# Attention scores of four heads in one step, with 64-row and 32-row products side by side, in a two-layer decoder trunk

## The chip, the cores and the metric

The kernel runs on one core of one Trainium2 chip. The metric is the device time of one launch in microseconds (us); the time given for a kernel is the median of its runs. One run is also recorded with the hardware profiler. Its trace gives each instruction of the engines: TensorE (PE, with its weight loads as PEld), VectorE (DVE), ScalarE (ACT), GpSimd (POOL), and the DMA queue that SyncE (SP) feeds.

## The reference

The reference is a trunk of two decoder layers over 16 learned meta tokens and 256 tokens (L = 272), width 1024. A layer is a half-step SwiGLU feed-forward net, a mixing sub-layer with two branches (latent attention and a gated recurrence, HGRN2), and a second feed-forward net. The last layer computes no queries for the meta tokens, since they are dropped at the end. The change is in the attention branch:

```python
def mla(c_q, c_kv, k_pe, pos, q_norm_w, kv_norm_w, w_uq, w_ukv):
    H, DQK = MLA_HEADS, QK_NOPE + QK_ROPE          # 8 heads, 64 + 32
    q = (rms_norm(c_q, q_norm_w) @ w_uq).reshape(B, L, H, DQK)
    q = jnp.concatenate([q[..., :QK_NOPE], rope(q[..., QK_NOPE:], pos)], axis=-1)
    kv = (rms_norm(c_kv, kv_norm_w) @ w_ukv).reshape(B, L, H, QK_NOPE + V_HEAD)
    v = kv[..., QK_NOPE:]
    k_rot = rope(k_pe[:, :, None, :], pos)
    k = jnp.concatenate([kv[..., :QK_NOPE], jnp.broadcast_to(k_rot, (B, L, H, QK_ROPE))], axis=-1)
    ...
        s = jnp.einsum('bqhd,bkhd->bhqk', qi, k).astype(jnp.float32) * scale
        s = jnp.where(k_pos[None, :] <= q_pos[:, None], s, NEG_BIG)
        p = jax.nn.softmax(s, axis=-1).astype(v.dtype)
        return jnp.einsum('bhqk,bkhd->bqhd', p, v)
```

A score is thus a dot product over 96 numbers: 64 "nope" numbers that each head has for itself, in the queries and in the keys, and 32 "rotary" numbers, whose keys are the same for all heads.

## The kernel before

Activations lie with channels on the 128 partitions and tokens along the free axis. Every weight product is done as three fp32r products of split operands (`mm3`, lines 163 to 165), and the weights stream from memory in pieces of 128 x 1024. `piece()` (line 151) hands out the next piece and prepares the one two further on: an ACT cast (`wh`, line 144) and a DVE subtraction (`wl`, line 145). The attention's own products (scores, transposes, values) and those of the recurrence are plain fp32.

There are eight PSUM banks in two pools of four: "mm" for weight products, "aux" for everything small: scores, transposes of the softmax, the recurrence's blocks.

`mix` (line 398) is one layer's mixing sub-layer. `heads()` (line 474) makes queries, keys and values. For each head it copies the 64 nope rows and the 32 rotary rows into a tile of its own: `qs[hd]` holds rows 0 to 95 of the queries (copies on lines 486 and 500), `kT[hd]` the same of the keys (lines 512 and 513, the second a copy of the shared rotary key `kpe`). `attention()` (line 612) then works head by head. `scores(hd)` does two score products of 96 rows, one for each block of 128 queries (144 and 272 keys), each in an "aux" bank of its own: mask add (642), row maximum (644), exponential with row sum (645), reciprocal (646), scaling of the 16 meta columns into `pmc` (647) and of the rest (650 on ACT, 652 on DVE). `turn(hd)` transposes the probabilities (658 to 660) and copies them to `ptt` (662). In layer 0 alone a small softmax of the 16 meta queries comes first (lines 617 to 632). At the end come the transposes of the meta columns of all heads into `pmt` (675 to 677), and the values in two rounds of two banks: one product of 128 rows with `vt[0]`, a block-diagonal tile of all heads' meta values (682), and the products with the token values (687).

Three generators run interleaved: attention (a), the recurrence (r: `halving()`, then `outputs()`) and weight products (w: the gates' tiles, then projections). `weave("awr", ...)` (line 889) takes one step of each in turn, up to the next `yield`. A scheduler in the compiler orders the instructions within each engine's queue, and each engine then works through its queue in that order. Within the recurrence these places matter: the last products of `halving()` (775 and 778); in `outputs()` the products with meta values (793, 794), the mean square over a head's channels (809, tile `ss`; 811 reads it), its inverse root (lines 283 to 288), and the products that spread it over the partitions (817, "rowsel"), in four "aux" banks, read on line 819.

Of the kernel before, what the change touches and what calls it, by code (L numbers as in the profile page):

```python
# [10 lines left out]
F32 = mybir.dt.float32  # L11
F32R = mybir.dt.float32r
# [15 lines left out]
H = 8  # L28
# [24 lines left out]
def trunk(ctx: ExitStack, tc: tile.TileContext, a: dict):  # L53
# [344 lines left out]
    def mix(l, norm, nxt):  # L398
# [9 lines left out]
        pe = slice(64, 96)  # L408
# [63 lines left out]
        qs, kT, vt = [], [], []  # L472

        def heads():
# [3 lines left out]
            qs.extend(act() for _ in range(H))  # L478
            for pr in range(4):
# [4 lines left out]
                for j in range(2):  # L484
                    js = slice(j * 64, j * 64 + 64)
                    S.copy(out=qs[2 * pr + j][0:NOPE, cq], in_=ps[js, cq])
            yield
            for g in range(2):
# [4 lines left out]
                qp, qw = tmp(), tmp()  # L493
# [4 lines left out]
                for j in range(4):  # L498
                    js = slice(j * 32, j * 32 + 32)
                    S.copy(out=qs[4 * g + j][pe, cq], in_=qp[js, cq])  # L500
# [3 lines left out]
            kT.extend(act() for _ in range(H))  # L504
            for pr in range(4):
# [4 lines left out]
                for j in range(2):  # L510
                    js = slice(j * 64, j * 64 + 64)
                    S.copy(out=kT[2 * pr + j][0:NOPE], in_=ps[js, ca])
                    S.copy(out=kT[2 * pr + j][pe], in_=kpe[0:32])
# [98 lines left out]
        def attention():  # L612
            pmt = act()
            pmc = T([P, 2, P], F32, "pmc", 1)
            sm = T([P, 2, H, 3], F32, "sm", 1)
            if not last:
                ps = PS("aux")
                for hd in range(H):
                    E.matmul(ps[0:NM, hd * NM:(hd + 1) * NM], qs[hd][0:DQK, 0:NM], kT[hd][0:DQK, 0:NM],
                             start=True, stop=True)  # L620
                pmm = T([NM, H, NM], F32, "pmm", 1)
                smm = T([NM, 2, H], F32, "smm", 1)
                V.tensor_tensor(out=pmm, in0=ps[0:NM, 0:P].rearrange("p (h s) -> p h s", s=NM),
                                in1=causal[0:NM, 0:NM].unsqueeze(1).broadcast_to([NM, H, NM]), op=ALU.add)
# [10 lines left out]
            def scores(hd):  # L635
                pms[hd] = [T([P, L], F32, "pm", 4) for _ in range(2)]
                for i, n in enumerate((144, L)):
                    pmx = pms[hd][i]
                    ps = PS("aux")
                    E.matmul(ps[:, 0:n], qs[hd][0:DQK, TOK[i + 1][0]:TOK[i + 1][1]], kT[hd][0:DQK, 0:n],  # L640
                             start=True, stop=True)
# [23 lines left out]
            for hd in range(H):  # L665
                scores(hd)
                if hd:
                    turn(hd - 1)
                yield
# [320 lines left out]
```

## Time and profile before

| | |
|---|---|
| median of 3 runs | 1221.21 us (1219.85 to 1221.59) |
| profiled execution | 1220.78 us |
| its span, first to last instruction | 1218.8 us |
| PE, DVE, ACT busy | 1203.2, 866.9, 645.5 us |
| read from memory | 200.89 MB, 166 GB/s over the span |

The span begins with the first instruction of the program, and the profiled execution is 2.0 us longer. In layer 0 `heads()` runs from about 295 us and the weave of attention, recurrence and gates from 317 to some 375 us; in layer 1 the same parts lie at about 901 and 921 to 976 us. A row of a group (`line engine op out<-in xcount | busy, mean | idle before`) gives the time of all its instructions and the mean of one in ns; a row of the timeline gives start, time, engine, line and operation. A plain fp32 product is one instruction of the program but two in the trace.

### The profile page before, as it was taken

Reading aid. Unit: us, or ns where it says so; the run is one execution under the profiler, and the core shown is the slowest. Engines: PE = TensorE matmul, PEld = TensorE weight load, DVE = VectorE, ACT = ScalarE, POOL = GpSimd, SP = SyncE. Lnnn points to the kernel's source line nnn. Section 1 sums busy time; section 2 is a strip of 40 time slices with the busy share of each in tenths; the row PEclk is TensorE's granted clock in tenths of the full one; section 3 lists DMA queues with packets and bytes.
Section 4 is the critical chain, followed back from the end, with each engine's and each line's share of the span. In section 5 each row is a group of like instructions: output and inputs, shape, how many; then the busy total and the mean of one; then the engine's idle time right before and its main releaser. Section 6 shows DMA issues by size and latency. Waiting matters only on the chain.

```text
span 1218.8 us, 24265 instructions
## 1 busy us (share of the span) xinstructions
PE 1203.2 (99%) x10210; PEld 1170.0 (96%) x10210; DVE 866.9 (71%) x1522; ACT 645.5 (53%) x1067; POOL 8.7 (1%) x19
## 2 busy tenths in 40 slices
PE   7999999999999999999999999999999999999997
PEld 6999999999989999999999999999998899999986
DVE  6877755788786877776558777558877777877643
ACT  5544444575784554444445444445767745544442
POOL 0000000000000000000000000000000000000000
PEclk9999999999999999999999999999999999999999
DMA  7646565544534554646555555556454444655651
GB/s 227 201 149 205 166 189 158 177 143 131 173 105 139 173 163 152 205 153 210 159 165 180 174 173 194 171 173 177 143 151 128 151 156 162 208 173 173 208 190 52
DMA packets 188781, 203.50 MB, mean 167 GB/s; under 512 B 3349, under 2 KB 176481, under 8 KB 188673
## 3 DMA queue, kind: packets, MB, share of 16 engines
q1 hardware_dynamic: 188272, 201.36, 52.0%
q8 instruction: 80, 1.31, 0.5%
q10 hardware_dynamic: 400, 0.60, 0.2%
q14 instruction: 29, 0.23, 0.1%
HBM read 200.89 MB, written 1.05 MB: 166 GB/s over the span
## 4 chain that ended last, share of the span: by engine, by line
PE 96%; DVE 2%; ACT 1%; DMA 0%; issue 0%; SPq 0%; POOLq 0%; POOL 0%
PE pmm L163 22%; PE pmm L164 21%; PE pmm L165 21%; PE paux L164 7%; PE paux L165 7%; PE paux L163 7%; PE pmm L372 2%; PE pmm L373 2%; PE pmm L374 2%; PE paux L640 1%; DVE wl L145 1%; PE paux L711 1%; DMA raw<-x 0%; PE paux L687 0%; PE pmm L376 0%; PE paux L682 0%
## 5 line engine op out<-in xcount | busy, mean ns | idle before, releaser
L144 ACT CAST wh<-raw 128x1024 fp32r<-128x1024 f32 (+3 forms) x398 | 398.4, 1006 | 395.3 <-PE pmm L164 275.6
L145 DVE TENSOR_TENSOR wl<-raw,wh 128x1024 fp32r<-128x1024 f32 (+3 forms) x398 | 465.5, 1173 | 178.9 <-ACT wh L144 176.9
L163 PE MATMUL pmm<-x,wh 128*128 128x272 f32 (+1 forms) x1312 | 382.3, 292 | 0.0
L164 PE MATMUL pmm<-x,wh 128*128 128x272 f32 (+1 forms) x1312 | 376.0, 287 | 0.0
L165 PE MATMUL pmm<-x,wl 128*128 128x272 f32 (+1 forms) x1312 | 375.9, 287 | 0.0
L163 PEld LDWEIGHTS pmm<-x,wh 128*128 128x128 f32 x1312 | 246.7, 188 | 2.2 <-issue 0.7
L164 PEld LDWEIGHTS pmm<-x,wh 128*128 128x128 f32 x1312 | 247.1, 188 | 1.0
L165 PEld LDWEIGHTS pmm<-x,wl 128*128 128x128 f32 x1312 | 246.5, 188 | 0.3
L163 PE MATMUL pmm<-act,wh 128*128 128x272 f32 (+1 forms) x836 | 239.7, 287 | 0.6 <-DVE act L605 0.6
L165 PE MATMUL pmm<-act,wl 128*128 128x272 f32 (+1 forms) x836 | 238.8, 286 | 0.4 <-DVE wl L145 0.4
L164 PE MATMUL pmm<-act,wh 128*128 128x272 f32 (+1 forms) x836 | 238.8, 286 | 0.0
L163 PE MATMUL paux<-x,wh 128*128 128x272 f32 (+1 forms) x704 | 201.1, 286 | 0.0
L164 PE MATMUL paux<-x,wh 128*128 128x272 f32 (+1 forms) x704 | 201.1, 286 | 0.0
L165 PE MATMUL paux<-x,wl 128*128 128x272 f32 (+1 forms) x704 | 201.1, 286 | 0.0
L163 PEld LDWEIGHTS pmm<-act,wh 128*128 128x128 f32 x836 | 157.3, 188 | 0.9 <-DVE act L605 0.8
L165 PEld LDWEIGHTS pmm<-act,wl 128*128 128x128 f32 x836 | 157.0, 188 | 0.6 <-DVE wl L145 0.6
L164 PEld LDWEIGHTS pmm<-act,wh 128*128 128x128 f32 x836 | 157.4, 188 | 0.0
L163 PEld LDWEIGHTS paux<-x,wh 128*128 128x128 f32 x704 | 132.8, 189 | 0.0
L164 PEld LDWEIGHTS paux<-x,wh 128*128 128x128 f32 x704 | 132.6, 188 | 0.0
L165 PEld LDWEIGHTS paux<-x,wl 128*128 128x128 f32 x704 | 132.5, 188 | 0.0
L168 ACT CAST act<-tmp 128x272 fp32r<-128x272 f32 (+1 forms) x88 | 36.5, 415 | 122.5 <-DVE tmp L316 122.5
L312 DVE TENSOR_TENSOR tmp<-pmm,rstd 128x272 f32<-128x272 f32 (+1 forms) x88 | 38.3, 435 | 52.8 <-PE pmm L165 52.7
(249 smaller groups left out, 1037.4 us busy)
## 6 DMA issues: line engine op xcount, KB each, us to landing
raw<-ffn_w_gu SPq DMA_DIRECT2D x86, 1024.0 KB, 5.2
raw<-w_in SPq DMA_DIRECT2D x36, 1024.0 KB, 5.4
raw<-ffn_w_down SPq DMA_DIRECT2D x34, 1024.0 KB, 5.4
raw<-ffn_w_down SPq DMA_DIRECT2D x12, 768.0 KB, 4.9
raw<-w_out SPq DMA_DIRECT2D x8, 1024.0 KB, 5.3
raw<-w_proj_attn SPq DMA_DIRECT2D x4, 1024.0 KB, 5.1
raw<-w_proj_rec SPq DMA_DIRECT2D x4, 1024.0 KB, 5.1
raw<-ffn_w_gu SPq DMA_DIRECT2D x4, 512.0 KB, 8.5
```

The lines of the kernel that those rows point to most:

```text
L144: S.copy(out=hw, in_=x)
L145: V.tensor_tensor(out=lw, in0=x, in1=hw.bitcast(F32), op=ALU.subtract)
L163: E.matmul(ps, wh, xh, start=start, stop=False)
L164: E.matmul(ps, wh, xl, start=False, stop=False)
L165: E.matmul(ps, wl, xh, start=False, stop=stop)
L168: S.copy(out=hi_tile[:, c], in_=src)
L312: V.tensor_tensor(out=gt[:, c], in0=pg[:, c], in1=r[:, c], op=ALU.mult)
L372: E.matmul(pst[t], ah[:, ts_], wh, start=k == 0, stop=False)
L373: E.matmul(pst[t], al[:, ts_], wh, start=False, stop=False)
L374: E.matmul(pst[t], ah[:, ts_], wl, start=False, stop=k == NF - 1)
L640: E.matmul(ps[:, 0:n], qs[hd][0:DQK, TOK[i + 1][0]:TOK[i + 1][1]], kT[hd][0:DQK, 0:n], start=True, stop=True)
L711: E.matmul(pv[32 * b:32 * b + 32, g, ti], k[:, g, bs], q[:, g, bs], start=True, stop=True)
```

## The change

Nothing of the mathematics changes; the score sum is split into its nope and its rotary part.

- **Queries and keys.** No head has tiles of its own any more. `qn[pr]` holds the nope rows of two heads (64 each), `kn[pr]` those of the keys, `qr[g]` the rotary rows of four heads (32 each); they are copied whole or not at all. `kpe` is copied three times, to rows 32, 64 and 96.
- **Scores of four heads.** `scores(h4)` takes four "aux" banks, one for each head; both query blocks of a head lie in its bank (columns 0 to 143 and 144 to 415). Two helpers, `nope` and `rotary`, multiply 64 and 32 rows; neighbours in the order use different rows of TensorE's array and different banks.
- **Meta scores** (layer 0): likewise, in four banks, with four mask adds for one.
- **Steps.** Attention has two steps of scores, each followed by an empty step and two of transposes, in place of eight of a head each. `pm` has 8 buffers for 4.
- **Meta values.** `vt[0]` and `pmt` are multiplied in four slices of 32 rows, one bank each, and the values come in one round of four banks.

```diff
-                for j in range(2):
-                    js = slice(j * 64, j * 64 + 64)
-                    S.copy(out=qs[2 * pr + j][0:NOPE, cq], in_=ps[js, cq])
+                qn.append(act())
+                S.copy(out=qn[pr][:, cq], in_=ps[:, cq])
...
-                for j in range(4):
-                    js = slice(j * 32, j * 32 + 32)
-                    S.copy(out=qs[4 * g + j][pe, cq], in_=qp[js, cq])
+                qr.append(qp)
...
-                for j in range(2):
-                    js = slice(j * 64, j * 64 + 64)
-                    S.copy(out=kT[2 * pr + j][0:NOPE], in_=ps[js, ca])
-                    S.copy(out=kT[2 * pr + j][pe], in_=kpe[0:32])
+                kn.append(act())
+                S.copy(out=kn[pr], in_=ps[:, ca])
+                if pr:
+                    S.copy(out=kpe[32 * pr:32 * pr + 32], in_=kpe[0:32])
...
+            def nope(ps, hd, ts_, n, first):
+                js = slice(hd % 2 * 64, hd % 2 * 64 + 64)
+                E.matmul(ps, qn[hd // 2][js, ts_], kn[hd // 2][js, 0:n], start=first, stop=False)
+
+            def rotary(ps, hd, ts_, n, second):
+                js = slice(hd % 4 * 32, hd % 4 * 32 + 32)
+                E.matmul(ps, qr[hd // 4][js, ts_], st["kpe"][js, 0:n], start=False, stop=second)
...
-            def scores(hd):
-                pms[hd] = [T([P, L], F32, "pm", 4) for _ in range(2)]
-                for i, n in enumerate((144, L)):
-                    pmx = pms[hd][i]
-                    ps = PS("aux")
-                    E.matmul(ps[:, 0:n], qs[hd][0:DQK, TOK[i + 1][0]:TOK[i + 1][1]], kT[hd][0:DQK, 0:n],
-                             start=True, stop=True)
...
+            def scores(h4):
+                pss = [PS("aux") for _ in range(4)]
+                where = ((0, 144), (144, L))
+                for h2 in (0, 2):
+                    for i, (o, n) in enumerate(where):
+                        for j in (h2, h2 + 1):
+                            nope(pss[j][:, o:o + n], h4 + j, slice(*TOK[i + 1]), n, i == 0)
+                for i, (o, n) in enumerate(where):
+                    for j in range(4):
+                        rotary(pss[j][:, o:o + n], h4 + j, slice(*TOK[i + 1]), n, i == 1)
+                for j in range(4):
+                    hd = h4 + j
+                    pms[hd] = [T([P, L], F32, "pm", 8) for _ in range(2)]
+                    for i, (o, n) in enumerate(where):
+                        pmx, ps = pms[hd][i], pss[j][:, o:o + n]
...
-            for hd in range(H):
-                scores(hd)
-                if hd:
-                    turn(hd - 1)
+            for h4 in (0, 4):
+                scores(h4)
                 yield
-            turn(H - 1)
-            yield
+                yield
+                for h2 in (0, 2):
+                    turn(h4 + h2)
+                    turn(h4 + h2 + 1)
+                    yield
...
+            pss = [PS("aux") for _ in range(4)]
+            for pr, ps in enumerate(pss):
+                js = slice(32 * pr, 32 * pr + 32)
+                E.matmul(ps[:, cq], vt[0][js, pr * P:(pr + 1) * P], pmt[js, cq], start=True, stop=False)
```

The scheduler's order shows what the change does to the queues. Line numbers after the change are those of the changed file. In layer 0 PE's queue had, for one head (here the second), two products of 96 rows in two banks (`paux_679`, `paux_680`), with the first head's transposes behind them:

```order
L640 MATMUL paux_679_4128<-act_628_3852,act_592_3593 128x144
L640 MATMUL paux_680_4136<-act_628_3852,act_592_3593 128x272
L658 MATMUL paux_681_4144<-ident_1_61,pm_665_4057 128x128
L659 MATMUL paux_681_4144<-ident_1_61,pm_666_4058 128x128
L660 MATMUL paux_681_4144<-ident_1_61,pm_666_4058 128x128
```

For heads 0 to 3 it now has the nope products in pairs (L614), then the rotary products in fours (L618), over the banks `paux_660` to `paux_663`; the last four, of 272 columns, are left out here:

```order
L614 MATMUL paux_660_4042<-act_624_3842,act_592_3602 128x144
L614 MATMUL paux_661_4043<-act_624_3842,act_592_3602 128x144
L614 MATMUL paux_660_4042<-act_624_3842,act_592_3602 128x272
L614 MATMUL paux_661_4043<-act_624_3842,act_592_3602 128x272
L614 MATMUL paux_662_4044<-act_626_3851,act_594_3614 128x144
L614 MATMUL paux_663_4045<-act_626_3851,act_594_3614 128x144
L614 MATMUL paux_662_4044<-act_626_3851,act_594_3614 128x272
L614 MATMUL paux_663_4045<-act_626_3851,act_594_3614 128x272
L618 MATMUL paux_660_4042<-act_469_2762,act_607_3728 128x144
L618 MATMUL paux_661_4043<-act_469_2762,act_607_3728 128x144
L618 MATMUL paux_662_4044<-act_469_2762,act_607_3728 128x144
L618 MATMUL paux_663_4045<-act_469_2762,act_607_3728 128x144
```

Two products a head become four, and all four "aux" banks are taken together.

The second place is DVE's queue in layer 0, from the recurrence's mean square (L811, after the change L828) on. `paux_725` and `paux_726` are the two blocks of head 4's scores, `wl` is weight preparation, L284 the long reciprocal of the inverse root:

```order
L811 TENSOR_SCALAR tmp_721_4334<-paux_720_4329 128x272
L642 TENSOR_TENSOR paux_725_4339<-paux_725_4339,cst_3_68 128x128
L145 TENSOR_TENSOR wl_744_4424<-raw_730_4362,wh_743_4423 128x1024
L644 TENSOR_REDUCE sm_661_4038<-paux_725_4339 128x1
L642 TENSOR_TENSOR paux_726_4347<-paux_726_4347,cst_3_68 128x128
L284 RECIPROCAL tmp_734_4394<-tmp_734_4394 128x272
L646 RECIPROCAL sm_661_4038<-sm_661_4038 128x1
L644 TENSOR_REDUCE sm_661_4038<-paux_726_4347 128x1
L647 TENSOR_SCALAR pmc_660_4037<-pm_723_4337,sm_661_4038 128x16
L652 TENSOR_SCALAR pm_723_4337<-pm_723_4337,sm_661_4038 128x128
```

After the change the banks of heads 4 to 7 are `paux_716` to `paux_719`. Between L828 and these rows stand only one weight row and the long reciprocal, which L286 reads:

```order
L286 TENSOR_TENSOR tmp_734_4442<-tmp_733_4441 128x272
L657 TENSOR_TENSOR paux_716_4332<-paux_716_4332,cst_3_68 128x128
L287 SCALAR_TENSOR_TENSOR tmp_734_4442<-tmp_734_4442,tmp_714_4329 128x272
L659 TENSOR_REDUCE sm_653_4009<-paux_716_4332 128x1
L657 TENSOR_TENSOR paux_717_4333<-paux_717_4333,cst_3_68 128x128
L657 TENSOR_TENSOR paux_718_4334<-paux_718_4334,cst_3_68 128x128
L659 TENSOR_REDUCE sm_653_4009<-paux_717_4333 128x1
L659 TENSOR_REDUCE sm_653_4009<-paux_718_4334 128x1
L657 TENSOR_TENSOR paux_719_4335<-paux_719_4335,cst_3_68 128x128
L659 TENSOR_REDUCE sm_653_4009<-paux_719_4335 128x1
L661 RECIPROCAL sm_653_4009<-sm_653_4009 128x1
L657 TENSOR_TENSOR paux_716_4332<-paux_716_4332,cst_3_68 128x128
```

The long reciprocal now stands ahead of the first mask add, and a head's second add (the last row, `paux_716` again) stands behind the reciprocal of its first block (L661 for L646), which needs ACT's exponential. The inverse root's last row (L288) comes 34 rows after L828 where it came 26 rows after L811, since more of the heads' softmax lies between.

The third place is PE's queue at the rowsel products (L817) in layer 0. Before, all four stand together, 64 weight products and the scores and transposes of two heads after the mean square:

```order
L165 MATMUL pmm_764_4508<-x_390_2335,wl_732_4365 128x272
L163 MATMUL pmm_764_4508<-x_393_2343,wh_731_4364 128x272
L817 MATMUL paux_746_4456<-act_722_4335,cst_3_68 128x272
L817 MATMUL paux_747_4457<-act_722_4335,cst_3_68 128x272
L817 MATMUL paux_748_4458<-act_722_4335,cst_3_68 128x272
L817 MATMUL paux_749_4459<-act_722_4335,cst_3_68 128x272
L640 MATMUL paux_760_4486<-act_633_3857,act_597_3598 128x144
L640 MATMUL paux_761_4494<-act_633_3857,act_597_3598 128x272
```

After, three stand together behind 65 weight products and the scores of four heads (`paux_739` to `paux_741`), and the fourth follows 12 weight products later, with the first transposes of heads 4 to 7 behind it:

```order
L164 MATMUL pmm_755_4519<-x_394_2344,wh_730_4411 128x272
L834 MATMUL paux_739_4479<-act_715_4330,cst_3_68 128x272
L834 MATMUL paux_740_4480<-act_715_4330,cst_3_68 128x272
L834 MATMUL paux_741_4481<-act_715_4330,cst_3_68 128x272
L165 MATMUL pmm_755_4519<-x_393_2343,wl_731_4412 128x272
L163 MATMUL pmm_755_4519<-x_413_2515,wh_730_4411 128x272
```

```order
L164 MATMUL pmm_764_4564<-x_348_1984,wh_736_4446 128x272
L834 MATMUL paux_742_4482<-act_715_4330,cst_3_68 128x272
L673 MATMUL paux_751_4507<-ident_1_61,pm_720_4352 128x128
L674 MATMUL paux_751_4507<-ident_1_61,pm_721_4353 128x128
L675 MATMUL paux_751_4507<-ident_1_61,pm_721_4353 128x128
L165 MATMUL pmm_764_4564<-x_347_1983,wl_737_4447 128x272
L673 MATMUL paux_753_4513<-ident_1_61,pm_722_4366 128x128
```

The transposes that stood between the groups of weight products have moved behind the rowsel products.

71 lines of the change are left out of this document (33 added, 38 removed).

## The prediction

> **What bounds the kernel now.** I read the page first: busy shares, then the chain that ended last. Then I read the stretches of layer 0 in which attention, the gated recurrence ("rec") and the gate projections are woven together, then the waits.
>
> ```profile
> span 1218.8 us, 24265 instructions
> PE 1203.2 (99%) x10210; PEld 1170.0 (96%) x10210; DVE 866.9 (71%) x1522; ACT 645.5 (53%) x1067; POOL 8.7 (1%) x19
> PE 96%; DVE 2%; ACT 1%; DMA 0%; issue 0%; SPq 0%; POOLq 0%; POOL 0%
> 345.00:360.00 15.00, 14.43 (x115) 13.51 (x114) 14.59 (x45) 11.04 (x29) 0.00 (x0) 1.00 0.26 95
> 375.00:395.00 20.00, 20.00 (x162) 20.00 (x161) 14.72 (x25) 8.64 (x11) 0.00 (x0) 1.00 0.49 158
> ```
>
> TensorE (PE) is the bound: 96% of the chain. A microsecond taken from PE's own work is a microsecond gained, and one that PE stands waiting is lost for good, because nothing after it has slack. But VectorE (DVE), 71% busy over the span, is 14.59 of 15.00 us busy at 345 to 360 us, where rec meets the softmax, against 14.72 of 20.00 afterwards. PE is off it by a hair there.
>
> **PE's own work.** The terms come from the chain in order of time and one group:
>
> ```profile
> 27.52 0.46 PE paux L272 x2
> 317.01 0.49 PE paux L619 x16
> 329.48 0.71 PE paux L640 x4
> 349.75 0.71 PE paux L817 x8
> 364.42 0.92 PE paux L682 x4
> 965.99 0.86 PE paux L682 x4
> L640 PE MATMUL paux<-act,act 96*128 96x144 f32 (+1 forms) x64 | 14.9, 354 | 1.1 <-DVE act L819 1.1
> ```
>
> An fp32 product shows as two instructions. One of 128 rows and 272 columns takes 0.46 us (L272). Four products of 32 rows in four row groups and four banks (L817) take 0.71 us together, not 4 x 0.46 = 1.84: side by side works, at an entry price of 0.71 - 0.46 = 0.25 us.
>
> *Scores.* One head (144 and 272 columns) is 0.71 us (L640), four heads 2.84. Afterwards two pairs of nope products and one rotary foursome cost three such times, 2.13, plus entries into the 64-row and the 32-row shape, 0.50: 2.63. That saves 0.2 per four heads, 0.8 in all. No product of 64 rows is in this trace. Lower bound: a pair costs one product, as the four of L817 nearly do; upper bound: it costs two, +1.4 per four heads, +5.6 in all. I take the lower, L817 being the nearest row.
>
> *Values' meta products.* 0.92 twice in layer 0 (L682), 0.86 twice in layer 1, become one L817-like 0.71 each: 1.13 + 1.01 = 2.1 us saved.
>
> *Meta scores* (layer 0 only): eight products take 0.49 (L619). Sixteen narrower ones cost between 0.49 (all side by side) and 0.98 + 0.50 (none, and two entries); I take 1.0, so 0.5 lost.
>
> *A wait that goes.* L640 now sits behind the hand-over of L817's banks, 1.1 us over both layers; no scores stand there any more.
>
> PE by itself: -0.8 - 2.1 + 0.5 - 1.1 = **-3.5 us**.
>
> **What leaves ACT.** Per layer 8 + 8 + 8 + 8 part-tile copies become 4 + 0 + 4 + 3:
>
> ```profile
> L513 ACT COPY act<-act 32x272 f32<-32x272 f32 x16 | 6.7, 417 | 0.3
> L500 ACT COPY act<-tmp 32x272 f32<-32x272 f32 (+1 forms) x16 | 6.6, 410 | 1.6 <-DVE tmp L497 1.4
> L512 ACT COPY act<-pmm 64x272 f32<-64x272 f32 x16 | 6.1, 382 | 0.2
> L486 ACT COPY act<-pmm 64x272 f32<-64x272 f32 (+1 forms) x16 | 6.0, 374 | 3.6 <-PE pmm L165 3.5
> ```
>
> 5 x 0.417 + 8 x 0.410 + 4 x 0.382 + 4 x 0.374 = 8.4 us of ACT per layer. I cost it at nothing: PE runs beside these copies. Below nothing by at most 0.5, should DVE's weight rows come sooner.
>
> **The new waits.** One bank per score becomes four banks at a time, and "aux" has four. From a group of scores to the end of its softmax every other user of "aux" waits: the recurrence's last blocks after the first group, the rowsel products (L834, before L817) after the second. And a head's two blocks now share a bank: the second block's mask add stands on DVE behind the first block's reciprocal, which waits for ACT's exponential. Here is DVE from the recurrence's mean square (L811) to its inverse root (L288), which rowsel multiplies:
>
> ```profile
> 338.80 0.67 PE L809 MATMUL paux<-tmp,ones 128*32 128x272 f32 x8
> 349.68 0.74 PE L817 MATMUL paux<-act,cst 32*128 32x272 f32 x8
> 339.60:348.90 9.30, 9.30 (x73) 9.09 (x73) 9.30 (x28) 8.65 (x18) 0.00 (x0) 1.00 0.35 114
> 339.58 0.44 DVE L811 TENSOR_SCALAR tmp<-paux 128x272 f32<-128x272 f32 x1 [0.24 <-PE paux L809]
> 341.28 0.30 DVE L644 TENSOR_REDUCE sm<-paux 128x1 f32<-128x144 f32 x1
> 341.70 1.84 DVE L284 RECIPROCAL tmp<-tmp 128x272 f32<-128x272 f32 x1
> 343.48 0.42 DVE L644 TENSOR_REDUCE sm<-paux 128x1 f32<-128x272 f32 x1
> 344.50 0.48 DVE L642 TENSOR_TENSOR paux<-paux,cst 128x128 f32<-128x128 f32 x2
> 348.52 0.43 DVE L288 SCALAR_TENSOR_TENSOR act<-tmp,tmp 128x272 f32<-128x272 f32 x1
> 341.14 0.43 ACT L283 ACTIVATE tmp<-tmp 128x272 f32<-128x272 f32 x1
> 341.59 1.28 ACT L645 ACT_TABLE_LOAD   x1
> 342.88 0.38 ACT L645 ACTIVATE pm<-paux,sm 128x144 f32<-128x144 f32 x1
> 343.16 0.19 ACT L645 ACTIVATION_READ_ACCUMULATOR pm<-paux,sm 128x1 f32 x1
> 344.56 0.50 ACT L645 ACTIVATE pm<-paux,sm 128x272 f32<-128x272 f32 x1
> L645 ACT ACTIVATION_READ_ACCUMULATOR pm<-paux,sm 128x1 f32 x32 | 6.3, 198 | 0.0
> L642 DVE TENSOR_TENSOR paux<-paux,cst 128x128 f32<-128x128 f32 x32 | 8.5, 289 | 0.0
> L145 DVE TENSOR_TENSOR wl<-raw,wh 128x1024 fp32r<-128x1024 f32 (+3 forms) x398 | 465.5, 1173 | 178.9 <-ACT wh L144 176.9
> L647 DVE TENSOR_SCALAR pmc<-pm,sm 128x16 f32<-128x16 f32 x32 | 7.3, 229 | 0.5
> L652 DVE TENSOR_SCALAR pm<-pm,sm 128x128 f32<-128x128 f32 x16 | 4.4, 277 | 0.0
> L646 DVE RECIPROCAL sm<-sm 128x1 f32<-128x1 f32 x32 | 4.9, 155 | 1.7 <-ACT pm L645 1.4
> ```
>
> From 339.58 to 348.95 DVE works without a gap: 9.37 us. Two adds in one row take 0.48 where the mean is 0.289, so an instruction's step is its time less some 0.09. Afterwards the same path holds three more adds (3 x 0.20), two short reductions and one long (2 x 0.21 + 0.33), one more reciprocal (0.07), meta scaling (0.14) and block scaling (0.19): 1.75 us.
>
> It also holds waits. (1) Now an add, a weight row and a reduction hide the square root, which ends at 341.57, 1.99 after L811 starts. Afterwards only L811 and one weight row stand ahead of the long reciprocal, 0.35 + 1.13: 0.5 idle. (2) Now the exponential's table load (1.28) runs beside that 1.84 us reciprocal. Afterwards it waits for the first reduction, behind it: 1.28 + 0.38 + 0.19 = 1.85 until the first small reciprocal, against three adds and three reductions, 0.60 + 0.75: 0.5 idle. (3) Each second block's reduction is followed by its exponential and read-out, 0.50 + 0.20, before DVE can divide; beside it stands some 0.35 of a gate tile's scaling: 0.35 idle, three heads, 1.0. The path is 9.37 + 1.75 + 2.0 = 13.1.
>
> PE's cover between the two products is 0.67 + 2.63 + 65 weight products. A product's step is 0.125 (rows from 17.74 on, below), so 8.1, in sum 11.4. The inverse root is ready (339.58 - 338.80) + 13.1 = 13.9 after L809's counterpart starts: PE waits 2.5. Now it is ready at 0.78 + 9.37 = 10.15 and PE comes at 10.88: 0.7 to spare, which is why the row of L817 has no wait. The fourth rowsel product needs the bank that the first one's consumer frees, on DVE nine rows further (reciprocals, scalings, an add, a reduction, one weight row: 2.3, and its own 0.5), against 0.7 + 12 x 0.125 = 2.2 on PE: 0.6 more. **Per layer 3.1**; bounds 0 (the cover suffices) and 4.
>
> *First four heads.* The first bank is free after add 0.20, reduction 0.30, table and exponential 1.85, then 0.07 + 0.20 + 0.14 + 0.19 + 0.42 and the second exponential 0.70: 4.1 us. PE has 26 weight products ahead of the next user in layer 1, about 3.1 (columns 256 for 272): 1.0 wait. In layer 0 the table is loaded for the meta softmax, but nine small DVE rows of that and a weight row stand ahead, so it comes to as much. For the later banks DVE also has gate tiles and weight rows to do; I take 0.6. **Per layer 1.6**; bounds 0 and 3.
>
> **Sum.** 2 x (3.1 + 1.6) - 3.5 = **+5.9 us** on the profiled execution's 1220.8 (span 1218.8 and 2.0 around it). The median shown is 1221.2, 0.4 away. I predict **1226.5**.
>
> **Rivals.**
>
> *Faster: the waits stay hidden.* Place: DVE between mean square and inverse root. If that path stays within PE's cover, 11.4 - 0.8 = 10.6 us, that is, if the added 1.75 and the idle 2.0 shrink to 1.2, and the first banks come within 3.1, then only PE's -3.5 remains: **1217.3**. For it: the copies that leave ACT may let weight rows come earlier. Against it: DVE has no gap there now. Chance 0.14. Halfway, waits of 3 or 4 us cancel the gain, **1221**: 0.12.
>
> *Slower still: a nope pair isn't side by side.* Then the change doesn't do what it says: 2 x 0.71 per pair, +5.6: **1232**. Against it: L817 (32 rows). Chance 0.07.
>
> *Slower still: PE loses its pace in the new waits.*
>
> ```profile
> 16.99 0.43 PE L165 MATMUL pmm<-x,wl 128*128 128x272 f32 x1
> 17.22 0.43 PE L163 MATMUL pmm<-x,wh 128*128 128x272 f32 x1
> 17.74 0.29 PE L164 MATMUL pmm<-x,wh 128*128 128x272 f32 x1
> 17.86 0.29 PE L165 MATMUL pmm<-x,wl 128*128 128x272 f32 x1
> ```
>
> At the start of the program the products step at 0.23 us, later at 0.125, though the clock column has 1.00 throughout. A return to 0.23 for some 4 us costs 4 x (1 - 0.125/0.23) = 1.8 us; with one return per layer, at rowsel, **1230**. It decides from a wait that is long enough; of before, none is over 1 us after the start, and PE kept its pace. Chance 0.07. The Trainium skill, "TensorE: Matmul & The Clock Gate", section "Why this matters for your kernels", sets the limit at idle gaps of about 3 us; no run here shows it, and by that rule the waits forecast here fall just short.
>
> **How the numbers follow.** Forecast 0.60, 1223.5 to 1230 by its own bounds; rivals 0.14, 0.12, 0.07, 0.07. The range of 8 in 10 leaves out the hidden waits and half of the serial pairs: 1219.5 to 1232.5. A measurement of this kernel tells about 0.2%, 2.4 us, from no change: faster 0.14, same 0.12, slower 0.74.
>
> **What would show it.** After the change PE should sit idle 2 to 3 us ahead of L834, released by DVE's L288 or ACT's exponential, and about 1 us ahead of L792, once per layer. DVE should show gaps ended by ACT between L661 and L657. Four L618 products of 272 columns should start within 0.1 us, and the pair of L614 likewise. L699 should take 0.7 us for all four. I am wrong if L834 waits under 1 us, or if pairs of L614 follow each other at 0.45 us.

## The result and the profile after

The changed kernel takes **1228.46 us** (median of 4 runs, 1228.29 to 1228.48) against 1220.7 for the kernel before on the same chip: a ratio of **1.0064**, 95% interval 1.0052 to 1.0076. It is 7.8 us slower. The profiled execution took 1228.48 us.

The page after: the span, the busy times, and the row of the granted clock (one digit for each fortieth of the span).

```profile
span 1226.7 us, 24377 instructions
PE 1205.1 (98%) x10290; PEld 1170.1 (95%) x10290; DVE 867.1 (71%) x1525; ACT 625.6 (51%) x1025; POOL 8.6 (1%) x19
PEclk9999999999989999999999999999999999999999
```

ACT is 20 us less busy, 17 of them in the copies (25.4 us in the prediction's four rows, 8.2 in three now); DVE is as it was, and PE is 1.9 us busier in a span that is 7.9 longer. The one 8 in the clock row, in the slice from 337 to 368 us, is new. Stretches around the rowsel products in both layers, after the change (start:end, length, busy time of PE, PEld, DVE, ACT and POOL with the number of instructions, granted clock, DMA share, GB/s):

```profile
345.00:360.00 15.00, 12.59 (x77) 11.09 (x76) 12.96 (x46) 10.85 (x29) 0.00 (x0) 0.80 0.28 96
350.70:354.11 3.41, 1.14 (x9) 0.82 (x10) 3.41 (x13) 2.84 (x9) 0.00 (x0) 1.00 0.02 5
354.11:357.53 3.42, 3.42 (x14) 2.47 (x12) 2.30 (x9) 1.83 (x4) 0.00 (x0) 0.50 0.59 185
357.53:360.94 3.41, 3.41 (x17) 3.41 (x17) 2.73 (x7) 2.30 (x6) 0.00 (x0) 0.50 0.32 124
...
958.27:961.68 3.41, 0.82 (x9) 0.37 (x7) 3.41 (x12) 3.38 (x11) 0.00 (x0) 1.00 0.00 0
961.68:965.10 3.42, 3.42 (x16) 3.13 (x14) 2.95 (x11) 2.10 (x5) 0.00 (x0) 0.50 0.54 115
```

From 345 to 360 us PE was 14.43 us busy before, 12.59 now, at a mean clock of 0.80. A stretch in which PE is busy 1.14 or 0.82 of 3.41 us is followed by half clock: 6.83 us of it in layer 0, 3.42 in layer 1. At half clock weight products follow each other at 0.23 us (354.32, 354.55, 354.78) where the step is 0.125 at full clock. So nearly half of the time there is lost, an estimate of 3.4 + 1.7 = 5.1 us.

PE's timeline after, at the places the prediction named (start, time, engine, line, form, count, and in brackets the idle time before and who ended it):

```profile
315.97 0.37 PE L614 MATMUL paux<-act,act 64*16 64x16 f32 x16
316.26 0.28 PE L618 MATMUL paux<-act,act 32*16 32x16 f32 x16
...
322.79 0.71 PE L792 MATMUL paux<-gq,gk 128*128 128x128 f32 x4 [0.32 <-ACT pm L660]
...
339.61 1.68 PE L614 MATMUL paux<-act,act 64*128 64x144 f32 x16
341.22 0.98 PE L618 MATMUL paux<-act,act 32*128 32x144 f32 x16
342.13 0.39 PE L163 MATMUL pmm<-x,wh 128*128 128x272 f32 x1
...
352.97 0.73 PE L834 MATMUL paux<-act,cst 32*128 32x272 f32 x6 [2.41 <-ACT pm L660]
...
366.47 0.74 PE L699 MATMUL paux<-act,vt 32*128 32x272 f32 x8
...
931.36 0.49 PE L792 MATMUL paux<-gq,gk 128*128 128x128 f32 x2 [0.96 <-ACT pm L660]
...
939.63 0.33 PE L673 MATMUL paux<-ident,pm 128*128 128x128 f32 x1 [0.81 <-DVE act L819]
...
961.09 0.71 PE L834 MATMUL paux<-act,cst 32*128 32x256 f32 x6 [2.59 <-DVE sm L661]
```

The waits stand where they were forecast: 2.41 and 2.59 us ahead of the rowsel products, 0.3 to 1.0 behind the first four heads. The bracket of L834 in layer 0 names ACT's exponential, which frees a bank, but the inverse root is ready at the same moment (352.87, below). DVE from the mean square to the inverse root, after:

```profile
339.80 0.44 DVE L828 TENSOR_SCALAR tmp<-paux 128x272 f32<-128x272 f32 x1 [0.24 <-PE paux L826]
...
341.81 1.85 DVE L284 RECIPROCAL tmp<-tmp 128x272 f32<-128x272 f32 x1 [0.44 <-ACT tmp L283]
...
346.79 0.16 DVE L661 RECIPROCAL sm<-sm 128x1 f32<-128x1 f32 x1 [0.51 <-ACT pm L660]
...
348.46 0.17 DVE L661 RECIPROCAL sm<-sm 128x1 f32<-128x1 f32 x1 [0.29 <-ACT pm L660]
...
352.44 0.43 DVE L288 SCALAR_TENSOR_TENSOR act<-tmp,tmp 128x272 f32<-128x272 f32 x1
```

The path is 352.87 - 339.80 = 13.07 us long, and 12.92 in layer 1.

### The profile page after: what moved, and what is told of

Its sections match the earlier page's. It is cut to its first block, busy times and chain, and to the rows that moved or that the text cites. A ratio compares the mean times of both kernels' runs of the same rounds, so it can differ in the third digit from the quotient of the medians.

```text
span 1226.7 us, 24377 instructions
## 1 busy us (share of the span) xinstructions
PE 1205.1 (98%) x10290; PEld 1170.1 (95%) x10290; DVE 867.1 (71%) x1525; ACT 625.6 (51%) x1025; POOL 8.6 (1%) x19
## 4 chain that ended last, share of the span: by engine, by line
PE 94%; DVE 3%; ACT 2%; issue 0%; DMA 0%; SPq 0%; POOLq 0%; POOL 0%; ACTq 0%
PE pmm L163 21%; PE pmm L165 21%; PE pmm L164 21%; PE paux L164 7%; PE paux L165 7%; PE paux L163 7%; PE pmm L374 2%; PE pmm L372 2%; PE pmm L373 2%; DVE wl L145 1%; PE paux L728 1%; ACT wh L144 0%; DMA raw<-x 0%; PE paux L704 0%; ACT pm L660 0%
```

## The experiments

Each ran beside the kernel before, which took 1220.2 to 1220.4 us in all four series.

**values_only** is the kernel before with the changed loop over the values:

```
-            for p2 in range(2):
...
+            pss = [PS("aux") for _ in range(4)]
+            for pr, ps in enumerate(pss):
+                js = slice(32 * pr, 32 * pr + 32)
+                E.matmul(ps[:, cq], vt[0][js, pr * P:(pr + 1) * P], pmt[js, cq], start=True, stop=False)
```

> The kernel before with the values' part of the change alone. Theory (the loss sits in the scores' part: the wait ahead of the row selectors and the low clock behind it, about 13 us, against some 5 us that the tensor engine saves): the values' meta products cost 0.7 us once instead of 0.92 us twice per layer, so 1.1 us per layer are saved, no new wait ahead of the row selectors, the clock stays at 0.999; 1218 to 1219.5, about 2.2 us under the kernel before. Rival (four banks at once make the values wait for banks): the products wait 1 us or more per layer and the time is that of before or above it, 1220.5 to 1222.

1217.37 us, ratio 0.9977 (0.9968 to 0.9986): 3.0 us faster than before, and the fastest kernel of the study. It beat its forecast of 1218 to 1219.5. If the parts add up, the 7.8 us of the whole are a gain of 3.0 here and a loss of 10.8 in the scores' part. In its PE timeline the rowsel products still wait for nothing, and the old wait of the scores behind them is still there:

```profile
350.08 0.74 PE L817 MATMUL paux<-act,cst 32*128 32x272 f32 x8
351.39 1.14 PE L640 MATMUL paux<-act,act 96*128 96x144 f32 x4 [0.57 <-DVE act L819]
```

**late_rowsel** is the changed kernel with one step more ahead of the rowsel products:

```
             yield from rsqrt(rg[:, cq], m[:, cq], cq)
+            yield
             pss = [PS("aux") for _ in range(G)]
```

> The changed kernel with one more yield ahead of the row selectors, so that one tile of dense products (3.05 us) and the transposes of two heads stand in front of them on the tensor engine. Theory (the vector engine's path to the inverse root is 13.1 us long and the tensor engine has 10.6 us of work beside it): the waits of 2.4 and 2.6 us go, with them the stretches at half clock (5 us); mean clock 0.999; 1218 to 1219.5, about 9 to 10 us under the changed kernel and 1 to 2 under the one before. Rival (the time is lost to the four-bank steps themselves, so that the wait only moves to the transposes or to the row selectors' banks): a wait of 2 us or more shows at the transposes or the row selectors, the clock still falls, 1226 or more.

1228.11 us, ratio 1.0062 (1.0048 to 1.0076): no gain, so the theory missed; the rival had time and place right, though not the size of the wait. Its PE timeline and stretches:

```profile
349.06 0.33 PE L673 MATMUL paux<-ident,pm 128*128 128x128 f32 x1
350.76 0.33 PE L674 MATMUL paux<-ident,pm 128*128 128x128 f32 x1 [1.38 <-ACT pm L665]
```

```profile
348.66:352.07 3.41, 1.93 (x13) 1.29 (x12) 3.08 (x14) 3.41 (x11) 0.00 (x0) 1.00 0.01 2
352.07:355.48 3.41, 3.34 (x16) 3.02 (x16) 3.41 (x13) 2.90 (x9) 0.00 (x0) 0.50 0.02 5
```

The rowsel products wait less, but the second group's transposes now stand first, and they wait for the softmax. The clock fell behind an idle time of only 1.38 us. So the inverse root is not the only thing that is late, and a wait far shorter than 2.4 us can be enough for the clock.

**rowsel_mm** takes the banks of the rowsel products from the other ring:

```
-            pss = [PS("aux") for _ in range(G)]
+            pss = [PS("mm") for _ in range(G)]
```

> The changed kernel with the row selectors' four banks taken from the dense tiles' ring instead of the ring that the scores use. Theory (the row selectors wait for the inverse root, the last of the vector engine's path): the wait in layer 0 stays within 0.2 us of 2.4, as the inverse root ended at 352.86 us and the last exponential at 352.88; the clock falls again; 1227 to 1230, where dense tiles that now wait for the row selectors' banks may add 1 to 2 us. Rival (the row selectors wait for the scores' banks): the wait and the low clock go, 1218 to 1221.

1230.55 us, ratio 1.0085 (1.0071 to 1.0099). The wait at the rowsel products is gone, as the rival said, but the time is not. PE's timeline, and DVE's last row of the inverse root:

```profile
350.05 0.33 PE L674 MATMUL paux<-ident,pm 128*128 128x128 f32 x1 [1.37 <-ACT pm L665]
...
352.22 0.48 PE L674 MATMUL paux<-ident,pm 128*128 128x128 f32 x1 [1.37 <-ACT pm L665]
...
353.05 1.29 PE L834 MATMUL pmm<-act,cst 32*128 32x272 f32 x8
...
352.30 0.43 DVE L288 SCALAR_TENSOR_TENSOR act<-tmp,tmp 128x272 f32<-128x272 f32 x1
```

With other banks the order on PE changed: 48 weight products stand between L826 and L834, not 65, and two transposes have come ahead. They wait 2 x 1.37 us instead. The inverse root still ends at 352.73, so the rowsel products could not have come much sooner with any banks: free banks did not shorten the path. Whichever taker of DVE's and ACT's late results comes first on PE pays.

**keep_pace** adds 24 products that nothing reads, ahead of the rowsel products:

```
+            fill = PS()
+            for k in range(24):
+                (xh, xl) = norm.parts[k % KD]
+                E.matmul(fill[:, cq], xh[:, 0:P], xh[:, cq], start=True, stop=True)
             pss = [PS("aux") for _ in range(G)]
```

> The changed kernel with 24 products of 272 columns (0.125 us each, 3.0 us) whose result nothing reads, written ahead of the row selectors; a scheduler then sets 17 products of a dense tile behind the row selectors that stood ahead of them. Theory (the clock falls because the tensor engine stood idle for 2.4 to 2.6 us): the work beside the vector engine's path is 9.0 instead of 8.1 us behind the scores, the idle time is 1.5 to 1.8 us, and the clock holds 1.0 behind it; the added work is 2 x 3.0 us less the 2 x 0.9 us of wait, the clock gives back 5.1 us: 1227 to 1228.5, the same as the changed kernel, with a mean clock of 0.999. Rival (the clock falls because of the narrow products, of 32 and 64 rows, which all stay): the half clock stays, 1232 or more.

1235.33 us, ratio 1.0123 (1.0109 to 1.0137): a miss again. The wait shrank to 1.58 us in layer 0 as reckoned, and to 2.0 in layer 1; a second one of 1.07 came up, and the clock fell for two stretches in each layer. Time and clock are those of the rival, which blames the narrow products; the next run speaks against it. In layer 0:

```profile
353.11 0.73 PE L838 MATMUL paux<-act,cst 32*128 32x272 f32 x6 [1.58 <-ACT pm L660]
...
355.79 0.82 PE L838 MATMUL paux<-act,cst 32*128 32x272 f32 x1 [1.07 <-DVE act L840]
```

```profile
351.07:354.48 3.41, 1.83 (x15) 1.25 (x13) 3.41 (x15) 2.61 (x8) 0.00 (x0) 1.00 0.00 0
354.48:357.89 3.41, 2.34 (x8) 1.40 (x7) 2.77 (x10) 2.50 (x5) 0.00 (x0) 0.50 0.71 208
```

**late_scores** puts the second group's scores behind the rowsel products:

```
                     turn(h4 + h2 + 1)
                     yield
+                if not h4:
+                    yield
+                    yield
```

> The changed kernel with two more yields behind the first group's transposes, so that the scores of the second four heads come behind the row selectors; on the tensor engine 58 dense products (7.2 us) then stand between the sums of squares and the row selectors, and no score of the second group stands ahead of the inverse root on the vector engine. Theory now (a step of four heads lays some 2.2 us per head of softmax on the vector engine and ScalarE, and what stands behind it there, the inverse root or the transposes, comes late): the inverse root takes about 5 us and the row selectors wait for nothing; the second group then meets no other chain, as the first group does, whose transposes wait for under 1 us; no stretch at half clock; 1216 to 1219. Rival (four heads in one step are late wherever they stand): the second group's transposes wait for 1.4 us or more in each layer, the clock falls behind them, 1223 or more.

1224.21 us, ratio 1.0031 (1.0019 to 1.0043): the rival's time, but without its wait of 1.4 us and its low clock. All the narrow products are still there, and in the profiled execution the clock is 1.00 in every stretch of both layers. What is left are smaller waits, the scores for the rowsel products' banks and the transposes for the softmax:

```profile
348.25 0.51 PE L614 MATMUL paux<-act,act 64*128 64x144 f32 x2 [0.76 <-DVE act L839]
...
962.06 0.33 PE L674 MATMUL paux<-ident,pm 128*128 128x128 f32 x1 [1.02 <-ACT pm L665]
```

**four96** keeps the steps of four heads and goes back to 96 rows a head:

```
+                for j in range(4):
                     for i, (o, n) in enumerate(where):
...
+                        E.matmul(pss[j][:, o:o + n], qs[h4 + j][0:DQK, TOK[i + 1][0]:TOK[i + 1][1]],
+                                 kT[h4 + j][0:DQK, 0:n], start=True, stop=True)
```

> The changed kernel with the products of before: each head's 96 rows (nope and rotary in one tile, the copies on ScalarE that this needs, the meta scores in one bank), but four heads in one step with both blocks of a head in one bank, and the values as changed. Theory (the step of four heads makes the wait, the wait makes the low clock): the wait ahead of the row selectors stays at 2 us or more and the stretches at half clock stay; the scores cost some 0.5 us more per layer and the ends of the meta scores 0.1; 1227 to 1231. Rival (products of 32 and 64 rows make the clock fall): the wait may stay, the clock holds 1.0, 1222 to 1225.

1220.02 us, ratio 0.9996 (0.9987 to 1.0005): below both forecasts. Neither the wait nor the low clock is there, though four banks are taken at once and both blocks of a head share one. PE's timeline:

```profile
353.78 0.77 PE L826 MATMUL paux<-act,cst 32*128 32x272 f32 x6
...
356.17 0.72 PE L826 MATMUL paux<-act,cst 32*128 32x272 f32 x2
...
956.25 0.87 PE L826 MATMUL paux<-act,cst 32*128 32x256 f32 x6
```

The rowsel products start at 353.8, hardly later than the 352.97 of the changed kernel, but PE did 84 weight products since the sums of squares (87 in layer 1) where the changed kernel has 65 (67). Nineteen steps of 0.125 us are 2.4 us, the wait of the changed kernel. DVE's path is nearly the same: 12.62 us in layer 0, 12.91 in layer 1. Nearly the same readiness, another order.

**adds_first** writes a step's mask adds and maxima ahead of its first exponential:

```
                 for j in range(4):
                     hd = h4 + j
+                    for i, (o, n) in enumerate(where):
+                        ps = pss[j][:, o:o + n]
+                        V.tensor_tensor(out=ps[:, n - P:n], in0=ps[:, n - P:n], in1=causal, op=ALU.add)
+                        V.tensor_reduce(out=sm[:, i, hd, 0:1], in_=ps, axis=AX.X, op=ALU.max, negate=True)
+                for j in range(4):
+                    hd = h4 + j
```

> The changed kernel with the mask additions and maxima of all eight blocks of a step written ahead of the first exponential, so that no addition stands behind a reciprocal that waits for ScalarE. Theory (the vector engine's gaps of 0.5 and 0.3 us behind the exponentials are part of its path of 13.1 us): the path shortens by 0.5 to 1 us, the wait ahead of the row selectors to 1.5 to 2 us, as the scheduler also sets 6 dense products fewer ahead of them (0.75 us); stretches at half clock shorten or stay; 1224 to 1228.5. Rival (the path is set by the work, not by its gaps): no change beside the changed kernel's 1228.5, or the first transposes wait longer, 1229 to 1231.

1223.09 us, ratio 1.0022 (1.0013 to 1.0031): 5.4 us under the changed kernel, better than forecast. The waits at the rowsel products are 1.75 and 2.01 us, the half clock one stretch per layer:

```profile
352.36 1.01 PE L838 MATMUL paux<-act,cst 32*128 32x272 f32 x8 [1.75 <-ACT pm L669]
...
956.29 0.73 PE L838 MATMUL paux<-act,cst 32*128 32x256 f32 x8 [2.01 <-DVE act L288]
```

Only 59 weight products stand ahead, six fewer (0.75 us), and still PE waits less. DVE's path is 11.66 us in layer 0, 1.41 shorter, and 2.41 + 0.75 - 1.41 = 1.75: the adds behind reciprocals, with the gaps ahead of them, were a real part of it.

**late_rowsel_turns** moves the rowsel products and the second group's transposes two steps back. **late_groups** moves the rowsel products by two and the transposes by one, and the first group, with all behind it, by one. The diff of the former:

```
             yield from rsqrt(rg[:, cq], m[:, cq], cq)
+            yield
+            yield
...
                 scores(h4)
                 yield
                 yield
+                if h4:
+                    yield
+                    yield
```

> The changed kernel with two more yields ahead of the row selectors and two more between the second group's scores and its transposes, all products as changed. On the tensor engine 96 dense products (12.0 us) then stand between the second group's scores and the row selectors; in the changed kernel 65 stand there (8.1 us), with the products of before in steps of four heads 83 (10.4 us). Theory now (the vector engine's path is 13 us long in all of these, and what differs is how much dense work stands ahead of whoever waits for it; the low clock follows from the idle time): no wait of more than 0.5 us at the row selectors or the transposes, clock 0.999, the first group's waits (0.5 and 0.4 us in layer 0, 1.1 and 1.0 in layer 1) stay: 1228.5 - 5.0 - 5.1 = 1218.4, range 1217 to 1220. Rival (products of 32 and 64 rows cost more than they save, which four96 left out): the waits go and the time is still 1221 or more.

> As the run with later row selectors and transposes, and the first group of four heads one round later too, behind the products of the recurrent part that waited for its banks (lines 792 and 795 of the changed kernel). Theory: those products no longer wait (0.5 and 0.4 us in layer 0, 1.1 in layer 1), 72 dense products stand ahead of the row selectors (9.0 us), behind an inverse root whose reciprocal now runs ahead of the second group's first addition: 1216.5, range 1215.5 to 1218. Rival (the waits move to the next taker of the banks, the products of lines 810 and 811 or the first transposes): 1218.5 or more.

1226.63 us (1.0045, 1.0033 to 1.0057) and 1226.81 (1.0058, 1.0038 to 1.0078): both missed, though late_groups' rival, that the waits move to the next taker, came true (the products of lines 810 and 811 wait for 0.8 us in layer 0 and 0.6 in layer 1). In the first, with 96 weight products ahead, the first three rowsel products wait for nothing in layer 0, but the fourth and the transposes, which take the same banks in turn, now follow each other without weight products between. PE in late_rowsel_turns:

```profile
355.23 0.73 PE L839 MATMUL paux<-act,cst 32*128 32x272 f32 x6
356.71 0.72 PE L839 MATMUL paux<-act,cst 32*128 32x272 f32 x2 [0.74 <-ACT pm L660]
358.67 0.33 PE L673 MATMUL paux<-ident,pm 128*128 128x128 f32 x1 [1.24 <-DVE act L841]
```

Dense work spent ahead of one taker is missing ahead of the next.

**held_selectors** sets, with all products as changed, nearly the PE order of four96 by hand; for that, the second group's transposes come two steps later, too:

```
+            st["mid"] = lambda: select(range(3))
+            yield
+            select(range(3, G))
```

(`select` issues rowsel products; `mid` is called half-way through the next weight tile, 84 weight products behind the scores.)

> All products as changed, but the row selectors are written where the run with before's products in steps of four heads had them on the tensor engine: three of them behind 84 dense products counted from the second group's scores (65 in the changed kernel), 12 more dense products, the fourth, then the transposes of two heads. Theory now (what decides is how much dense work the written order sets ahead of the row selectors and between them and the transposes, not the kind of product): no wait over 0.5 us at the row selectors in either layer, clock 0.998 or more, and the time of four96 (1220.0) less some 1 us that the products of 32 and 64 rows save, plus the first group's waits of layer 1 (some 1 us more than in four96): 1218.5 to 1221. Rival (the narrow products, or the order on the vector engine that comes with them, make the wait): 1.5 us or more of wait at the row selectors or the transposes, 1223 or more.

1223.53 us, ratio 1.0023 (1.0014 to 1.0032): above the forecast, within the rival's time, but with waits of some 1.1 us a layer, not the rival's 1.5. Of the 2.41 and 2.59 us, the first three rowsel products keep nothing in layer 0 and 0.59 us in layer 1; the fourth waits for 0.44 and 0.55 us, and in layer 0 the first transposes wait, too:

```profile
356.89 0.72 PE L842 MATMUL paux<-act,cst 32*128 32x272 f32 x2 [0.44 <-ACT pm L662]
358.23 0.33 PE L675 MATMUL paux<-ident,pm 128*128 128x128 f32 x1 [0.62 <-DVE act L848]
```

```profile
355.97:359.38 3.41, 2.35 (x14) 1.46 (x14) 3.41 (x9) 3.09 (x7) 0.00 (x0) 1.00 0.92 286
359.38:362.79 3.41, 3.41 (x17) 3.41 (x16) 2.70 (x6) 3.41 (x9) 0.00 (x0) 0.50 0.06 24
```

Its runs fall in two: five with a mean clock of 0.999 took 1221.5 to 1222.5 us, six with 0.997 took 1223.5 to 1224.6. In the profiled one a single stretch is at half clock, 3.41 us, which costs 1.7; the two sets lie 2.1 apart. One program, and the clock falls or doesn't.

**two_heads** takes two heads in a step, in two banks:

```
-                pss = [PS("aux") for _ in range(4)]
+                pss = [PS("aux") for _ in range(2)]
```

> The changed kernel's products, but two heads in a step instead of four (nope rows of two and rotary rows of two side by side, two banks a step, four steps), with one head's transposes in each of the next rounds. Theory (four heads at once leave the vector engine idle in the rounds of transposes and pile up behind: 17.1 us busy of 24 where the kernel before has 18.9): the vector engine's work is as even as before, 18.5 us or more busy in the same stretch, the row selectors wait for under 0.8 us, the clock holds 0.999. On the tensor engine two heads cost 0.8 (nope, half of the 1.61 of four) and about 0.95 (rotary, as four side by side) against 1.40 before, 1.4 us more per layer than values_only: 1217.4 + 2.8 = 1220.2, range 1219 to 1222. Rival (it is the narrow products, not the size of the step): a wait of 1.5 us or more and a low clock, 1224 or more.

1224.56 us, ratio 1.0034 (1.0021 to 1.0047). The clock is 1.00 throughout and no rowsel product waits, so the rival's mechanism is absent; but the time is the rival's, and DVE's 316 to 340 us hold 17.6 us of work, not 18.5 or more: that theory fell. PE:

```profile
340.06 0.97 PE L614 MATMUL paux<-act,act 64*128 64x144 f32 x8
340.97 0.97 PE L618 MATMUL paux<-act,act 32*128 32x144 f32 x8
...
352.89 0.33 PE L672 MATMUL paux<-ident,pm 128*128 128x128 f32 x1 [0.61 <-DVE act L834]
```

Rotary rows of two heads cost as much as those of four (0.97 and 0.98), so half of the rows stay empty. Summed over both layers from a step's first score to the next product, the scores take 15.5 us here, 10.1 in the changed kernel, and 11.3 before. The 1.1 us that the kernel before waits for L819 lies ahead of the first score and is not in the 11.3.

## Why the prediction was right, point by point

The time, 1228.46, lies inside 1219.5 to 1232.5 and on the side that held 0.74, 2.0 us above the forecast. The mechanism was the forecast's; one term that it left to a rival, as large as the waits at rowsel, came on top.

- **The wait ahead of rowsel: right in place and size.** DVE's path was forecast as 13.1 us and is 13.07, PE's wait as 2.5 and is 2.41 and 2.59. Of the three stalls in it, the square root (0.5, measured 0.44) and the table load (0.5, measured 0.51) are as reckoned; the second blocks' adds were reckoned as 1.0 in three heads and show 0.29 once. All of DVE's gaps in the path make 1.3 us for 2.0, and its work 11.7 for 11.1, so two errors cancel: that the sum fits to 0.1 us is in part luck. adds_first confirms that the adds cost something. The 0.6 for the fourth rowsel product isn't seen in this trace, where the 12 weight products ahead of it ran at half clock; in held_selectors, with as many, it is 0.44 and 0.55.
- **The wait is an order's doing.** The prediction took the order as given. four96 has nearly the same readiness with 19 weight products more ahead of rowsel, and no wait; held_selectors removes most of the wait with the changed products. So neither the narrow products nor four banks at a time make the whole loss by themselves; four96 is still 2.7 us above values_only.
- **First four heads: near.** 3.2 us in both layers were forecast; the rows show 0.32, 0.96 and 0.81, 2.1, and L795 in layer 0 waits 0.28 more for ACT.
- **PE's own work: near in sum, off in parts.** -3.5 was forecast. For the values it was -2.1; their products take 9.7 us before and 6.8 after, -2.9, and values_only gained 3.0 (1.7 to 3.9 by its interval). For the scores it was -0.8; they went from 11.3 to 10.1, -1.2, and the 0.71 us reckoned for a head of before is also the mean of the 16. The pairs do run side by side: two products of a pair start within 0.01 us, four rotary ones within 0.02, and four heads' nope and rotary take 342.13 - 339.61 = 2.52 us, under the 2.63 of the lower bound. The meta scores cost 0.51 (0.49 before), not 1.0. The 1.1 us of the old wait went as forecast. Left out was that rowsel products in groups of three and one pay the entry twice: in four96, at full clock, 0.70 + 0.65 us to the next product in layer 0, where four together take 0.73. That is 1.3 us over both layers. In all -2.9 - 1.2 - 1.1 + 1.3 = -3.9.
- **The rival "PE loses its pace" came true beside the forecast.** It was priced at 1.8 us per return and two returns; by the clock they cost 3.4 and 1.7. The steps of 0.23 us at the start of the program, its premise, are as long as those at half clock, and the trace's record of the granted clock begins only at 17.5 us, where they turn to 0.125. So the 1.00 that the prediction read ahead of that was no measurement. Its chance of 0.07 was too low, for its condition was wrong: it was held to need one long wait, about as long as those forecast or longer. In these runs how little PE does in a fixed stretch tells more (last section).
- **The sum with measured terms**: 5.0 (rowsel) + 2.4 (first group) + 5.1 (clock) - 3.9 = 8.6, against 7.8 (6.3 to 9.3 by its interval). The forecast's own terms come to 3.5 in this sum where 5.9 was forecast: its waits of 9.4 measured 7.4. The clock's 5.1, which it left out, is more than that error, so that it ends 2.0 from the measured time is in part luck.

What stays open: with PE's order alike, held_selectors waits 0.44 and 0.62 us in layer 0 where four96 waits for nothing. Their orders on DVE and ACT differ too, and these were not made alike. That narrow products alone do not make the clock fall, late_scores and two_heads show; that idle time alone does, the end of the program shows (last section).

## What to carry to other kernels

Where PE and DVE are both close to full, as from 345 to 360 us here, packing PE's products tighter only moves the wait: count the dense work that stands ahead of each taker of DVE's results, for the written order can cost more (2.4 us here) than the products save. Test the parts of a change apart: one half of this one was worth 3.0 us, and the other hid it. And price a wait of 1 to 3 us on PE with the clock behind it, which here cost as much again as the waits.

## What the runs showed of the hardware

**The clock goes by fixed stretches of 3.41 us.** In every run whose clock fell in the weave the half clock begins and ends on a grid of 3.413 us that runs through both layers (in the changed kernel 961.68 - 354.11 = 178 x 3.413) and lies otherwise in each run. Read on that grid, in the eight runs that lost clock in the weave, from 285 to 400 and 890 to 1000 us of each, all 15 full-clock stretches in which PE was busy for 2.35 us or less were followed by one at half clock; of those with 2.44 or more only two were (2.63 and 2.67, both in late_groups). The lowest and the nearest to the limit:

| run | stretch from | PE busy of 3.41 us | next stretch's clock |
|---|---|---|---|
| after | 958.27 | 0.82 | 0.50 |
| late_rowsel | 348.66 | 1.93 | 0.50 |
| held_selectors | 355.97 | 2.35 | 0.50 |
| late_rowsel | 928.92 | 2.44 | 1.00 |
| keep_pace | 931.32 | 2.46 | 1.00 |

In late_scores, which kept its clock, a stretch with 2.39 us (from 961.03) was followed by full clock. PE's busy time alone doesn't decide, though. At the end of the program only products of 128 rows and 512 columns run, and there stretches with 1.63 us (two_heads), 2.20 (keep_pace), 2.24 (after) and 2.26 (rowsel_mm) were followed by full clock; half clock came only behind stretches with 1.15 us or less (1.15 in late_scores, none in the changed kernel, whose rows follow):

```profile
1217.68:1221.10 3.42, 2.24 (x10) 1.50 (x8) 1.04 (x4) 1.83 (x5) 0.55 (x1) 1.00 0.00 0
1221.10:1224.51 3.41, 0.00 (x0) 0.00 (x0) 0.99 (x4) 0.87 (x2) 0.56 (x1) 1.00 0.66 256
1224.51:1226.70 2.19, 0.00 (x0) 0.00 (x0) 0.00 (x0) 0.00 (x0) 0.00 (x0) 0.50 0.21 80
```

So the limit near 2.4 us holds for the mixed work of the weave; what else goes into it stays open. An idle time of 1.4 us among thin products can cost 1.7 us more, while one of 0.96 us at 931 us in the changed kernel, split over two stretches, cost no clock. Why layer 0 of the changed kernel lost two stretches and layer 1 one isn't settled; the first of the two held the fourth rowsel product (356.27 us).

The Trainium skill, "TensorE: Matmul & The Clock Gate", section "What's actually happening", gives a free-running window of 3413 ns; the grid agrees. The section "Why this matters for your kernels" of the same page of the Trainium skill sets the limit at idle gaps of about 3 us. Here 2.4 us and, with thin work around, 1.4 us were enough, and the measurement decides.

**Side by side, four cost what two cost.** Two foursomes of rotary products of 32 rows take as long as two pairs (0.98 and 0.97 us), so a half-filled foursome is pure loss. Splitting a foursome into three and one costs PE nearly the time of a second foursome (0.70 + 0.65 us against 0.73).
